# Opening of a hybrid transformer layer on one core: seven accumulators in place of six, mod sums and transposes in one PSUM bank, the second block's columns in three parts, six empty row steps

## The chip, the cores and the metric

One core of one Trainium2 chip runs the kernel. The metric is the device time of one execution in microseconds (us); the median of three executions of the kernel before the change is 1300.45 us (1300.31 to 1301.47). Lower is better.

## What is computed

One layer on x of 512 rows (T) and 1024 columns (D), float32 throughout. A conditioning vector c gives nine rows of modulation, `mod = silu(c) @ w_ada + b_ada`, 1024 wide each. Then come a SwiGLU feed-forward block (FFN, half weight), a mixer that adds a chunked matrix LSTM and a causal attention with forget gates, and a second FFN, each behind an RMS norm that is scaled and shifted by rows of `mod`.

```python
def swiglu(u, w_in, w_out):
    a, b = jnp.split(u @ w_in, 2, axis=-1)
    return (jax.nn.silu(a) * b) @ w_out
```

The change touches the first norm and the first FFN: `u = rms_norm(x) * gain * (1 + mod row 1) + mod row 0`, and `u @ w_in`, where `w_in` is 1024 by 2 x 2816 (an a half and a b half). The 2816 columns of a half are 22 blocks of 128, called j = 0 to 21.

## The kernel before, in words

**Products.** A float32 product is made of three products of rounded parts: a tensor u is split in `uh` (high part) and `ul` (the rest), a weight in `wh` and `wl`; `wh*uh`, `wl*uh` and `wh*ul` are added in a PSUM bank (PSUM is where TensorE writes). The high part is made on ScalarE (ACT in the profile), the rest on VectorE (DVE). PSUM has two pools of four banks, `gbank()` and `tbank()`.

**Opening** (`start`, L940 to L1106). It makes the first norm and the columns j = 0, 1, 2 of both halves, in eight blocks k of 128 rows of `w_in`, while everything is still being loaded. SyncE (SP) issues the loads in order: x, then for each k `ada_load(k)` (tile `ar`: the two column groups k of rows 0 and 1 of `w_ada`, four DMAs of 256 KB) and `load(k)` (tile `raw`: two DMAs of 192 KB). PE (TensorE) first runs `fill(30)`, thirty transposes of an identity matrix whose result nobody reads. For k = 0 the rows of `mod` are made on PE (`mod0`, L988, one call for each of the two rows), for k = 1 partly on PE (`mod1`, L994) and partly on DVE, from k = 2 on on DVE: `mod_first` (L998, L1000) and seven `mod` steps (L1003), each one of eight row blocks of `ar` times c, summed in the tile `ac`. `sums(k)` (L1018, two calls, four matmuls in the profile) adds the 128 partitions of `ac` on PE. `affine` (L1020, L1021, on ACT) makes the scale and shift `m` from these. `turn(k)` (L977) transposes the normed x into a bank `bt`; `u_hi` (L1026, L1028, ACT) reads it with `m` and writes `uh[k]` and `uf`; `u_lo` (L1030, DVE) writes `ul[k]`. Every one of these stands in the written order on its engine (`pin`).

The main loop runs k = 0 to 7. A block has 18 matmuls (L1084): three products, each into six accumulators, four `g` banks and two `t` banks. Between them stand, for the next k, `turn` ahead of the eighth matmul and `sums` ahead of the thirteenth. Of the two `t` banks left, one (`cb`) holds all sums, the results of `mod0` and the fill, and one holds `bt`.

**After the opening** (`run`). The six accumulators become three blocks of h. `ffn_in` then makes j = 3 alone, an a and a b half in a slot each of 24 matmuls (`w_stat`), and nine pairs of j in four slots each: 38 slots. Every `slot()` also runs one step of `pair_weights`, the later steps that are due (`tick`), and, if the slot's number n has n % 10 below 8, one step of `ada`: 32 steps, eight for each of the `mod` rows 3, 4, 2 and 6, each a load of 512 KB and one DVE step (L325) of about 1.2 us. After the eighth step of a row, `later` puts its end on the following ticks: `fold` (L364, L368), `high` (L369), `low` (L372), `total`, `bias` (L379) and `put`. The output product `pair_out` follows: eleven pairs, 18 matmuls each (two weight tiles, `wh`/`wl` of 1024 and of 512 columns), one tick in each pair.

The scheduler of the language sets the order on the engines outside the opening, from its own estimates.

Of the kernel before, what the change touches and what calls it, by code (L numbers as in the profile page):

```python
# [11 lines left out]
F32 = mybir.dt.float32  # L12
# [8 lines left out]
P = 128  # L21
# [26 lines left out]
class Layer:  # L48
# [359 lines left out]
    def ffn_in(self, w_in, j0, hp, tp, slot):  # L408

        if j0 % 2:  # L410
            ps = []
            for o in (0, FF):
                wt = self.w_stat(w_in, o + j0 * P)
                slot()
                ps.append(self.gbank())
                self.gemm_stat(ps[-1], wt, 0, T)
            self.pair_h(self.pair_s(ps[0], 0, T, tp), ps[1], j0, 0, T, hp, tp)
            self.lo_after = None
            j0 += 1
# [520 lines left out]
    def start(self, st, tp):  # L940
# [28 lines left out]
        def fill(n):  # L969

            for i in range(n):
                pin(nc.tensor.transpose(cb[:, 384:512], self.ident, self.ident))
# [5 lines left out]
        def ada_load(k):  # L978

            ars[k] = st.tile([P, NK, 2, P], F32, name=self.nm("ar"), tag="ar", bufs=7)  # L980
            halves = [(v, i) for v in range(2) for i in (0, 4)] if k == 0 else [(v, i) for i in (0, 4) for v in range(2)]
            for v, i in halves:
                nc.sync.dma_start(ars[k][:, i:i + 4, v, :], w_ada[i * P:(i + 4) * P, v * D + k * P:v * D + (k + 1) * P]
                                  .rearrange("(i p) n -> p i n", p=P))
        def mod0(v):

            for i in range(NK):
                pin(nc.tensor.matmul(cb[:, 128 * (v + 1):128 * (v + 2)], ars[0][:, i, v, :], self.ccol[:, i:i + 1].to_broadcast([P, P]),  # L988
                                     start=i == 0, stop=i == NK - 1))
# [14 lines left out]
        sh = [P, 2, NJ0 * P]  # L1004
        def load(k):
            raws[k] = self.raw(sh, [(lambda t, i=i: t[:, i, :],
                                     w_in[k * P:(k + 1) * P, i * FF:i * FF + NJ0 * P]) for i in range(2)])
# [5 lines left out]
        def w_lo(k):  # L1013
            hi, lo = ws[k]
            pin(nc.vector.tensor_tensor(lo, raws.pop(k), hi, op=SUB))
        def sums(k):
            for v in range(2):
                pin(nc.tensor.matmul(cb[:, 2 * k + v:2 * k + v + 1], accs[k][:, v, :], self.one, start=True, stop=True))  # L1018
        def affine(k, m, c, b):
            pin(nc.scalar.activation(m[:, 0:1], c[0], AF.Identity, bias=b[0]))  # L1020
            pin(nc.scalar.activation(m[:, 1:2], c[1], AF.Identity, scale=self.colC[:, 8 + k:9 + k], bias=b[1]))  # L1021
        def u_hi(k):
            m = sp.tile([P, 2], F32, name=self.nm("m"), tag="m", bufs=4)
            c = (cb[:, 2 * k:2 * k + 1], cb[:, 2 * k + 1:2 * k + 2]) if k else (cb[:, 128:129], cb[:, 256:257])
            affine(k, m, c, base if k == 1 else (self.colC[:, 16 + k:17 + k], self.colC[:, 24 + k:25 + k]))
# [3 lines left out]
        def u_lo(k):  # L1029
            self.last_ul = pin(nc.vector.tensor_tensor(self.ul[k], ufs[k], self.uh[k], op=SUB))  # L1030
        for k in range(3):
            ada_load(k)
            load(k)
# [4 lines left out]
        acc_ps = [self.gbank() for _ in range(4)] + [self.tbank() for _ in range(2)]  # L1038
        cb = self.tbank()
        fill(30)  # L1040
# [11 lines left out]
        mod0(0)  # L1052
        turn(0, (0, 1))
        turn(1, (0, 1))
        mod0(1)
        turn(0, (2, 3))
        mod1()
        w_hi(0)
        w_lo(0)
        u_hi(0)  # L1060
        mc, mb = [sp.tile([P, 2], F32, name=self.nm("m"), tag="m", bufs=4) for _ in range(2)]
# [4 lines left out]
        pin(nc.vector.tensor_copy(mc, acc_ps[-1][:, 0:2]))  # L1066
        affine(1, mb, (mc[:, 0:1], mc[:, 1:2]), (self.colC[:, 17:18], self.colC[:, 25:26]))
        u_lo(0)
        mod(1, 4, 8)
        w_lo(1)  # L1070
        mod_first(2, True)
        for k in range(NK):
# [4 lines left out]
            wh, wl = ws[k]  # L1077
            for i, (p, b) in enumerate((p, b) for p in range(3) for b in range(2 * NJ0)):
                if n < NK and i == 7:
                    turn(n, range(NT) if k else (2, 3))  # L1080
                if n < NK and i == 12:
                    sums(n)
                s = slice(b // 2 * P, (b // 2 + 1) * P)
                pin(nc.tensor.matmul(acc_ps[b], (wl if p == 1 else wh)[:, b % 2, s], self.ul[k] if p == 2 else self.uh[k],  # L1084
                                     start=k == 0 and p == 0, stop=k == NK - 1 and p == 2))
# [496 lines left out]
    def run(self):  # L1582
# [11 lines left out]
        with tc.tile_pool(name="f1t", bufs=1) as tp:  # L1594
# [5 lines left out]
            with tc.tile_pool(name="f1h", bufs=1) as hp:  # L1600
                for j in range(NJ0):
                    self.pair_h(self.pair_s(acc_ps[2 * j], 0, T, tp), acc_ps[2 * j + 1], j, 0, T, hp, tp)
                new = lambda: [tp.tile([P, D], F32, name=self.nm("acc"), tag="xn", bufs=1)]
# [4 lines left out]
                def slot():  # L1608
# [3 lines left out]
                    if n % 10 < 8:  # L1612
                        next(ada, None)
                    n += 1
                self.ffn_in(A["ffn1_w_in"][0], NJ0, hp, tp, slot)
# [298 lines left out]
```

## Time and profile before

| what | value |
|---|---|
| median of three executions | 1300.45 us |
| the profiled execution, own time | 1301.22 us |
| its span in the trace | 1299.4 us |
| PE busy | 1286.9 us, 99% |
| DVE busy | 982.2 us, 76% |
| ACT busy | 657.0 us, 51% |
| first matmul of block 0 of the opening | 16.80 us |
| first matmul of j = 3 | 59.05 us |
| second slot (j = 3, b half) | 64.62 us |

Times in the trace count from the start of the span. A row of a timeline has the start, the duration, the engine, the line, the output and input tiles, and how many instructions it groups; in square brackets stands how long the engine had been idle and what ended that. The duration of one matmul overlaps with the next one: the distance of two starts is what counts. A row of the chain of waits has the start, the length and what the time was spent on.

### The profile page before, as it was taken

What the parts mean: (1) busy time and instruction counts of PE and PEld (TensorE: products, weight loads), DVE (VectorE), ACT (ScalarE), POOL (GpSimd) and SP (SyncE); (2) the same over time, 40 slices, a digit from 0 to 9 for tenths busy, and PEclk for the clock granted to TensorE, in tenths of its full rate; (3) what the DMA queues carried; (4) which work ended last, traced back from release to release, by engine and by line L of the source; (5) the groups of instructions that cost most, each with busy time, mean ns of one, the idle gap of its engine ahead of it and who ended that gap; (6) DMA issues with size and microseconds to landing.
All of it is one profiled execution on the core that took longest, in us unless ns stands there. A gap on an engine that the chain in (4) does not pass through costs nothing.

```text
span 1299.4 us, 17819 instructions
## 1 busy us (share of the span) xinstructions
PE 1286.9 (99%) x6241; PEld 1079.9 (83%) x6241; DVE 982.2 (76%) x1764; ACT 657.0 (51%) x1086; POOL 34.9 (3%) x73
## 2 busy tenths in 40 slices
PE   7999999999999999999999999999999999999998
PEld 6788888887889888888888888888898888888887
DVE  6887786678788878999997866778977656535787
ACT  5623333266467656666575886344683223223741
POOL 1000000000010001000001100000000000000000
PEclk9999999999999999999999999999999999999999
DMA  9999998755865634545456985876649767634574
GB/s 291 274 311 304 328 308 276 227 175 178 303 193 140 178 100 130 172 137 158 133 128 163 269 192 141 245 233 201 194 149 333 274 229 270 219 98 139 166 268 148
DMA packets 248330, 272.02 MB, mean 209 GB/s; under 512 B 57824, under 2 KB 185472, under 8 KB 248240
## 3 DMA queue, kind: packets, MB, share of 16 engines
q1 hardware_dynamic: 241104, 254.55, 63.8%
q0 software_dynamic: 2752, 8.45, 1.9%
q10 hardware_dynamic: 4384, 7.88, 1.9%
q8 instruction: 49, 0.80, 0.3%
q14 instruction: 41, 0.34, 0.1%
HBM read 227.77 MB, written 43.06 MB: 208 GB/s over the span
## 4 chain that ended last, share of the span: by engine, by line
PE 90%; DVE 5%; DMA 2%; ACT 2%; issue 1%; SPq 1%; DVEq 0%; ACTq 0%
PE g L144 23%; PE g L142 23%; PE g L143 23%; PE t L142 4%; PE t L144 4%; PE t L143 4%; PE g L1084 1%; PE t L1500 1%; PE t L1470 1%; PE t L1440 1%; PE t L1441 1%; PE t L1084 1%; DVE wl L760 1%; DMA ar<-in_w_ada_dram 1%; ACT wh L117 0%
## 5 line engine op out<-in xcount | busy, mean ns | idle before, releaser
L117 ACT ACTIVATE wh<-raw 128x1024 fp32r<-128x1024 f32 (+2 forms) x238 | 239.9, 1015 | 350.3 <-DMA raw<-in_ffn_w_in_dram 116.6
L119 DVE TENSOR_TENSOR wl<-raw,wh 128x1024 fp32r<-128x1024 f32 (+2 forms) x238 | 276.6, 1168 | 137.1 <-ACT wh L117 128.5
L142 PE MATMUL g<-uh,wh 128*128 128x512 f32 (+1 forms) x880 | 341.1, 388 | 0.2 <-ACT wh L117 0.2
L144 PE MATMUL g<-uh,wl 128*128 128x512 f32 (+1 forms) x880 | 340.1, 386 | 0.3 <-DVE wl L119 0.2
L143 PE MATMUL g<-ul,wh 128*128 128x512 f32 (+1 forms) x880 | 339.2, 386 | 0.0
L144 PEld LDWEIGHTS g<-uh,wl 128*128 128x128 f32 x880 | 165.3, 188 | 34.2 <-DVE wl L119 0.9
L142 PEld LDWEIGHTS g<-uh,wh 128*128 128x128 f32 x880 | 165.4, 188 | 33.5 <-ACT wh L117 0.6
L143 PEld LDWEIGHTS g<-ul,wh 128*128 128x128 f32 x880 | 165.5, 188 | 32.4
L142 PE MATMUL g<-wh,uh 128*128 128x512 f32 (+1 forms) x256 | 97.6, 381 | 0.0
L144 PE MATMUL g<-wh,ul 128*128 128x512 f32 (+1 forms) x256 | 96.6, 377 | 0.0
L143 PE MATMUL g<-wl,uh 128*128 128x512 f32 (+1 forms) x256 | 96.5, 377 | 0.0
L325 DVE SCALAR_TENSOR_TENSOR acc<-raw,ccol,acc 128x1024 f32<-128x1024 f32 (+1 forms) x49 | 54.8, 1129 | 52.8 <-DMA raw<-in_w_ada_dram 52.8
L143 PE MATMUL t<-wl,A 128*128 128x512 f32 x176 | 68.5, 389 | 0.0
L142 PE MATMUL t<-wh,A 128*128 128x512 f32 x176 | 68.5, 390 | 0.0
L144 PEld LDWEIGHTS g<-wh,ul 128*128 128x128 f32 x256 | 48.2, 188 | 8.9
L143 PEld LDWEIGHTS g<-wl,uh 128*128 128x128 f32 x256 | 48.3, 189 | 8.3
L142 PEld LDWEIGHTS g<-wh,uh 128*128 128x128 f32 x256 | 48.2, 188 | 8.2
L142 PE MATMUL g<-yh,wh 128*128 128x512 f32 x128 | 50.0, 390 | 0.0
L144 PE MATMUL g<-yh,wl 128*128 128x512 f32 x128 | 49.9, 389 | 0.0
L143 PE MATMUL g<-yl,wh 128*128 128x512 f32 x128 | 49.8, 389 | 0.0
L1451 ACT ACTIVATE S<-S,mn 128x128 f32<-128x128 f32 (+1 forms) x64 | 35.6, 558 | 27.1 <-DVE mn L1443 17.0
L465 ACT ACTIVATE A<-E 128x768 fp32r<-128x768 f32 x22 | 18.6, 847 | 53.8 <-DVE E L464 53.6
(403 smaller groups left out, 2294.8 us busy)
## 6 DMA issues: line engine op xcount, KB each, us to landing
raw<-in_ffn_w_in_dram SPq DMA_DIRECT2D x80, 512.0 KB, 4.2
raw<-in_w_ada_dram SPq DMA_DIRECT2D x48, 512.0 KB, 5.7
raw<-in_w_mix_dram SPq DMA_DIRECT2D x46, 512.0 KB, 4.2
sa<-in_ffn_w_out_dram SPq DMA_DIRECT2D x22, 512.0 KB, 6.4
sb<-in_ffn_w_out_dram SPq DMA_DIRECT2D x44, 256.0 KB, 5.7
ws<-sa SPq DMA_DIRECT2D x22, 512.0 KB, 3.8
ws<-sb SPq DMA_DIRECT2D x44, 256.0 KB, 4.4
raw<-ws SPq DMA_DIRECT2D x44, 256.0 KB, 3.8
```

The costliest lines, as they stand in the source:

```text
L117: nc.scalar.activation(hi, src, AF.Copy)
L119: self.last_lo = nc.vector.tensor_tensor(lo, src, hi, op=SUB)
L142: pin(mm(ps, lh, rh, start=start, stop=False, skip_group_check=on))
L143: pin(mm(ps, lh, rl, start=False, stop=False, skip_group_check=on))
L144: self.last_mm = pin(mm(ps, ll, rh, start=False, stop=stop, skip_group_check=on))
L325: nc.vector.scalar_tensor_tensor(a, r[:, s], c, a, op0=MUL, op1=ADD)
L465: nc.scalar.activation(A1[:, 0:3, :], E[:, 0:3, :], AF.Copy)
L760: self.pin(self.nc.vector.tensor_tensor(l, self.raws[n][c], h, op=SUB))
L1084: pin(nc.tensor.matmul(acc_ps[b], (wl if p == 1 else wh)[:, b % 2, s], self.ul[k] if p == 2 else self.uh[k], start=k == 0 and p == 0, stop ...
L1440: nc.tensor.matmul(ps[:, :w], q[:, s], k[:, :w], start=True, stop=False)
L1441: nc.tensor.matmul(ps[:, :w], q[:, s], kl[:, :w], start=False, stop=True)
L1451: nc.scalar.activation(S[:, ws], S[:, ws], AF.Exp, scale=-1.0, bias=m, accum_out=sm[:, qb:qb + 1])
```

## The change

The opening now has seven accumulators, four `g` and three `t` banks. The seventh takes the a half of j = 3. `raw` of a block has 512 + 384 columns (128x896 in place of 128x768), so each k loads 64 KB more. Block 0 still has 18 matmuls; the seventh accumulator's three products of k = 0 stand first in block 1, which has 24; blocks 2 to 7 have 21. The bank `cb` is gone: `mod0` writes into accumulators 4 and 5, `mod1` and `sums(1)` into the seventh, and from k = 2 on `sums` takes a bank of the ring that `bt` also uses, of which one bank is left. So `sums(k)` needs the reads of the bank by `u_hi(k - 1)` done, and `turn(k)` those of `affine(k)`, which is issued right behind `sums`. `fill` has 25 transposes in a bank of that ring. `mod0` runs for both rows back to back, then `turn(0)` whole; `mod1` and what follows it (the copy, its `affine`, the DVE steps up to `mod_first(2)`) stand behind block 0's third matmul; `turn(1)` is whole and inside block 0. `sums` stands ahead of a block's own matmul 13 (k = 0), 10 (k = 1 and later; counted from 0, without the three extra), `turn` ahead of 8 (k = 0) and 15 (later). `ar` of k = 1 comes in six DMAs. After the opening, `ffn_in` makes only the b half of j = 3: 37 slots. The slots 8, 9, 18, 19, 28 and 29 have no `ada` step, so 31 of the 32 steps stand in slots, and the last one, of row 6, in the first tick of `pair_out`.

The diff, cut:

```diff
-    def ffn_in(self, w_in, j0, hp, tp, slot):
+    def ffn_in(self, w_in, j0, hp, tp, slot, s=None):
 
         if j0 % 2:
-            ps = []
-            for o in (0, FF):
-                wt = self.w_stat(w_in, o + j0 * P)
-                slot()
-                ps.append(self.gbank())
-                self.gemm_stat(ps[-1], wt, 0, T)
-            self.pair_h(self.pair_s(ps[0], 0, T, tp), ps[1], j0, 0, T, hp, tp)
+            wt = self.w_stat(w_in, FF + j0 * P)
+            slot()
+            ps = self.gbank()
+            self.gemm_stat(ps, wt, 0, T)
+            self.pair_h(s, ps, j0, 0, T, hp, tp)
...
-                pin(nc.tensor.transpose(cb[:, 384:512], self.ident, self.ident))
+                pin(nc.tensor.transpose(fb[:, 0:P], self.ident, self.ident))
...
-            halves = [(v, i) for v in range(2) for i in (0, 4)] if k == 0 else [(v, i) for i in (0, 4) for v in range(2)]
-            for v, i in halves:
-                nc.sync.dma_start(ars[k][:, i:i + 4, v, :], w_ada[i * P:(i + 4) * P, v * D + k * P:v * D + (k + 1) * P]
+            parts = [(0, 4), (4, 8)] if k != 1 else [(0, 4), (4, 6), (6, 8)]
+            for v, (i, e) in [(v, q) for v in range(2) for q in parts] if k == 0 else [(v, q) for q in parts for v in range(2)]:
+                nc.sync.dma_start(ars[k][:, i:e, v, :], w_ada[i * P:e * P, v * D + k * P:v * D + (k + 1) * P]
                                   .rearrange("(i p) n -> p i n", p=P))
...
             for i in range(NK):
-                pin(nc.tensor.matmul(cb[:, 128 * (v + 1):128 * (v + 2)], ars[0][:, i, v, :], self.ccol[:, i:i + 1].to_broadcast([P, P]),
+                pin(nc.tensor.matmul(acc_ps[4 + v][:, 0:P], ars[0][:, i, v, :], self.ccol[:, i:i + 1].to_broadcast([P, P]),
...
-        sh = [P, 2, NJ0 * P]
+        sh, na = [P, (2 * NJ0 + 1) * P], (NJ0 + 1) * P
         def load(k):
-            raws[k] = self.raw(sh, [(lambda t, i=i: t[:, i, :],
-                                     w_in[k * P:(k + 1) * P, i * FF:i * FF + NJ0 * P]) for i in range(2)])
+            raws[k] = self.raw(sh, [(lambda t, i=i: t[:, i * na:na + i * NJ0 * P],
+                                     w_in[k * P:(k + 1) * P, i * FF:i * FF + (NJ0 + 1 - i) * P]) for i in range(2)])
...
+        def affine(k, m, c, b, vs=(0, 1)):
+            for v in vs:
+                pin(nc.scalar.activation(m[:, v:v + 1], c[v], AF.Identity, bias=b[v],
+                                         **({"scale": self.colC[:, 8 + k:9 + k]} if v else {})))
         def sums(k):
+            c = self.tbank() if k > 1 else acc_ps[-1][:, 8:10]
             for v in range(2):
-                pin(nc.tensor.matmul(cb[:, 2 * k + v:2 * k + v + 1], accs[k][:, v, :], self.one, start=True, stop=True))
-        def affine(k, m, c, b):
-            pin(nc.scalar.activation(m[:, 0:1], c[0], AF.Identity, bias=b[0]))
-            pin(nc.scalar.activation(m[:, 1:2], c[1], AF.Identity, scale=self.colC[:, 8 + k:9 + k], bias=b[1]))
+                pin(nc.tensor.matmul(c[:, v:v + 1], accs[k][:, v, :], self.one, start=True, stop=True))
+            ms[k] = sp.tile([P, 2], F32, name=self.nm("m"), tag="m", bufs=6)
+            affine(k, ms[k], (c[:, 0:1], c[:, 1:2]), base if k == 1 else col(k))
         def u_hi(k):
-            m = sp.tile([P, 2], F32, name=self.nm("m"), tag="m", bufs=4)
-            c = (cb[:, 2 * k:2 * k + 1], cb[:, 2 * k + 1:2 * k + 2]) if k else (cb[:, 128:129], cb[:, 256:257])
-            affine(k, m, c, base if k == 1 else (self.colC[:, 16 + k:17 + k], self.colC[:, 24 + k:25 + k]))
+            m = ms[k]
             pin(nc.scalar.activation(self.uh[k], bt[k], AF.Identity, scale=m[:, 1:2], bias=m[:, 0:1]))
...
             self.last_ul = pin(nc.vector.tensor_tensor(self.ul[k], ufs[k], self.uh[k], op=SUB))
+        ms = {}
+        col = lambda k: (self.colC[:, 16 + k:17 + k], self.colC[:, 24 + k:25 + k])
...
-        acc_ps = [self.gbank() for _ in range(4)] + [self.tbank() for _ in range(2)]
-        cb = self.tbank()
-        fill(30)
+        fb = self.tbank()
+        fill(25)
+        acc_ps = [self.gbank() for _ in range(4)] + [self.tbank() for _ in range(3)]
...
-        mod0(0)
-        turn(0, (0, 1))
-        turn(1, (0, 1))
-        mod0(1)
-        turn(0, (2, 3))
-        mod1()
         w_hi(0)
         w_lo(0)
+        ms[0], mc, mb = [sp.tile([P, 2], F32, name=self.nm("m"), tag="m", bufs=6) for _ in range(3)]
+        c0 = [acc_ps[4 + v][:, 0:1] for v in range(2)]
+        mod0(0)
+        affine(0, ms[0], c0, col(0), (0,))
+        mod0(1)
+        affine(0, ms[0], c0, col(0), (1,))
+        turn(0, range(NT))
         u_hi(0)
-        mc, mb = [sp.tile([P, 2], F32, name=self.nm("m"), tag="m", bufs=4) for _ in range(2)]
         base = mb[:, 0:1], mb[:, 1:2]
...
         mod(1, 3, 4)
-        pin(nc.vector.tensor_copy(mc, acc_ps[-1][:, 0:2]))
-        affine(1, mb, (mc[:, 0:1], mc[:, 1:2]), (self.colC[:, 17:18], self.colC[:, 25:26]))
-        u_lo(0)
-        mod(1, 4, 8)
-        w_lo(1)
-        mod_first(2, True)
+        def mod1_out():
+            mod1()
+            pin(nc.vector.tensor_copy(mc, acc_ps[-1][:, 0:2]))
+            affine(1, mb, (mc[:, 0:1], mc[:, 1:2]), col(1))
+            mod(1, 4, 6)
+            u_lo(0)
+            mod(1, 6, 8)
+            w_lo(1)
+            mod_first(2, True)
         for k in range(NK):
...
                 load(k + 3)
-            wh, wl = ws[k]
-            for i, (p, b) in enumerate((p, b) for p in range(3) for b in range(2 * NJ0)):
-                if n < NK and i == 7:
-                    turn(n, range(NT) if k else (2, 3))
-                if n < NK and i == 12:
+            todo = [(p, b, k) for p in range(3) for b in range(2 * NJ0 + (k > 0))]
+            if k == 1:
+                todo = [(p, 2 * NJ0, 0) for p in range(3)] + todo
+            for i, (p, b, m) in enumerate(todo):
+                if k == 0 and i == 3:
+                    mod1_out()
+                if n < NK and i == (13, 13, 10)[min(k, 2)]:
                     sums(n)
-                s = slice(b // 2 * P, (b // 2 + 1) * P)
-                pin(nc.tensor.matmul(acc_ps[b], (wl if p == 1 else wh)[:, b % 2, s], self.ul[k] if p == 2 else self.uh[k],
-                                     start=k == 0 and p == 0, stop=k == NK - 1 and p == 2))
+                if n < NK and i == (8, 18, 15)[min(k, 2)]:
+                    turn(n, range(NT))
+                c = b % 2 * na + b // 2 * P
+                pin(nc.tensor.matmul(acc_ps[b], ws[m][p == 1][:, c:c + P], self.ul[m] if p == 2 else self.uh[m],
+                                     start=m == 0 and p == 0, stop=m == NK - 1 and p == 2))
...
+                s3 = self.pair_s(acc_ps[2 * NJ0], 0, T, tp)
...
-                    if n % 10 < 8:
+                    if n not in (8, 9, 18, 19, 28, 29):
                         next(ada, None)
                     n += 1
-                self.ffn_in(A["ffn1_w_in"][0], NJ0, hp, tp, slot)
+                self.ffn_in(A["ffn1_w_in"][0], NJ0, hp, tp, slot, s3)
+                self.later(1, lambda: next(ada, None))
```

On PE, the start of the opening up to the fourth matmul of block 0, before (`ar_158` is k = 0, `ar_166` k = 1, `t_302` and `t_305` are `bt` of k = 0 and 1):

```order
L988 MATMUL t_215<-ccol,ar_158 128x128 x8
L977 MATMUL t_302<-ident,xn_272 128x128
L977 MATMUL t_302<-ident,xn_274 128x128
L977 MATMUL t_305<-ident,xn_272 128x128
L977 MATMUL t_305<-ident,xn_274 128x128
L988 MATMUL t_215<-ccol,ar_158 128x128 x8
L977 MATMUL t_302<-ident,xn_290 128x128
L977 MATMUL t_302<-ident,xn_292 128x128
L994 MATMUL t_214<-ccol,ar_166 128x1 x4
L1084 MATMUL g_209<-uh_193,wh_322 128x512
```

And after (`t_317` is `bt` of k = 0):

```order
L986 MATMUL t_241<-ccol,ar_158 128x128 x8
L986 MATMUL t_242<-ccol,ar_158 128x128 x8
L975 MATMUL t_317<-ident,xn_270 128x128
L975 MATMUL t_317<-ident,xn_272 128x128
L975 MATMUL t_317<-ident,xn_288 128x128
L975 MATMUL t_317<-ident,xn_290 128x128
L1093 MATMUL g_237<-uh_195,wh_292 128x512
L1093 MATMUL g_238<-uh_195,wh_292 128x512
L1093 MATMUL g_239<-uh_195,wh_292 128x512
L992 MATMUL t_243<-ccol,ar_166 128x1 x4
```

The second `mod0` now stands ahead of all transposes of k = 0, those of k = 1 are gone from here, and `mod1` (L994, now L992) moved behind three matmuls of block 0.

On PE inside block 1, from the second product of the first accumulator to its third, before (sums of k = 2 in `ac_349`, bank `t_215` is `cb`, `t_420` is `bt` of k = 2):

```order
L1084 MATMUL g_209<-uh_194,wl_335 128x512
L977 MATMUL t_420<-ident,xn_272 128x128
L977 MATMUL t_420<-ident,xn_274 128x128
L977 MATMUL t_420<-ident,xn_290 128x128
L977 MATMUL t_420<-ident,xn_292 128x128
L1084 MATMUL g_210<-uh_194,wl_335 128x512
L1084 MATMUL g_211<-uh_194,wl_335 128x512
L1084 MATMUL g_212<-uh_194,wl_335 128x512
L1084 MATMUL t_213<-uh_194,wl_335 128x512
L1084 MATMUL t_214<-uh_194,wl_335 128x512
L1018 MATMUL t_215<-one,ac_349 128x1 x2
L1084 MATMUL g_209<-ul_202,wh_334 128x512
```

And after, from the third matmul of the second product on (sums in `t_424`, `bt` in `t_435`):

```order
L1093 MATMUL g_239<-uh_196,wl_326 128x512
L1021 MATMUL t_424<-one,ac_355 128x1 x2
L1093 MATMUL g_240<-uh_196,wl_326 128x512
L1093 MATMUL t_241<-uh_196,wl_326 128x512
L1093 MATMUL t_242<-uh_196,wl_326 128x512
L1093 MATMUL t_243<-uh_196,wl_326 128x512
L1093 MATMUL g_237<-ul_204,wh_325 128x512
L975 MATMUL t_435<-ident,xn_270 128x128
L975 MATMUL t_435<-ident,xn_272 128x128
L975 MATMUL t_435<-ident,xn_288 128x128
L975 MATMUL t_435<-ident,xn_290 128x128
L1093 MATMUL g_238<-ul_204,wh_325 128x512
```

The sums now stand ahead of the fourth matmul of the second product and of the transposes, which stand behind the first matmul of the third; six matmuls follow the transposes before block 2 begins, where before six followed the sums.

On DVE, in `pair_out` where the low part `hl` of row 6's fold is made, before (counting `pair_out`'s pairs from 0, `wl_2494` of 1024 and `wl_2500` of 512 columns are pair 3's, `wl_2539` is pair 4's):

```order
L119 TENSOR_TENSOR wl_2494<-raw_2490,wh_2493 128x1024
L372 TENSOR_TENSOR hl_2462<-acc_2060,hl_2462 64x1024
L458 TENSOR_TENSOR R_2359<-g_2290,sl_2287 128x512
L467 TENSOR_TENSOR R_2359<-E_2345 128x256
L463 TENSOR_TENSOR E_2345<-E_2345,R_2359 128x256
L119 TENSOR_TENSOR wl_2500<-raw_472_2497,wh_2499 128x512
L464 TENSOR_TENSOR E_2345<-E_2345 128x256
L397 COPY sh_2506<-g_2504 128x8
L468 TENSOR_TENSOR R_2359<-R_2359,E_2345 128x256
L398 SCALAR_TENSOR_TENSOR G_2507<-g_2504,colA 128x8
L119 TENSOR_TENSOR wl_2539<-raw_2535,wh_2538 128x1024
```

And after (the first row is pair 3's, `wl_2535` and `wl_2541` are pair 4's, `wl_2574` is pair 5's; `sh` and `G` are columns made of row 3):

```order
L119 TENSOR_TENSOR wl_2494<-raw_474_2491,wh_2493 128x512
L119 TENSOR_TENSOR wl_2535<-raw_2531,wh_2534 128x1024
L397 COPY sh_2499<-g_2497 128x8
L398 SCALAR_TENSOR_TENSOR G_2500<-g_2497,colA 128x8
L372 TENSOR_TENSOR hl_2503<-acc_2087,hl_2503 64x1024
L456 TENSOR_TENSOR R_2353<-g_2284,sl_2281 128x512
L465 TENSOR_TENSOR R_2353<-E_2339 128x256
L461 TENSOR_TENSOR E_2339<-E_2339,R_2353 128x256
L119 TENSOR_TENSOR wl_2541<-raw_485_2538,wh_2540 128x512
L462 TENSOR_TENSOR E_2339<-E_2339 128x256
L119 TENSOR_TENSOR wl_2574<-raw_2570,wh_2573 128x1024
```

All of pair 3's `wl` and the first tile of pair 4's now stand ahead of `hl`, where half of pair 3's stood ahead of it before: one pair more.

Further down on DVE, the last of ten steps L492 (L490 after) that end earlier parts of the product, before (`wl_2580` and `wl_2586` are pair 5's, `wl_2618` is pair 6's):

```order
L119 TENSOR_TENSOR wl_2580<-raw_2576,wh_2579 128x1024
L119 TENSOR_TENSOR wl_2586<-raw_492_2583,wh_2585 128x512
L492 TENSOR_TENSOR Ra_2608<-Ra_1349,A_495_2607 128x512
L492 TENSOR_TENSOR Rb_2609<-Rb_1350,A_495_2607 128x512
L119 TENSOR_TENSOR wl_2618<-raw_2614,wh_2617 128x1024
```

And after (`wl_2615` is pair 6's):

```order
L490 TENSOR_TENSOR Rb_2526<-Rb_994,A_479_2524 128x512
L490 TENSOR_TENSOR Ra_2564<-Ra_1165,A_488_2563 128x512
L490 TENSOR_TENSOR Rb_2565<-Rb_1166,A_488_2563 128x512
L490 TENSOR_TENSOR Ra_2605<-Ra_1338,A_498_2604 128x512
L490 TENSOR_TENSOR Rb_2606<-Rb_1339,A_498_2604 128x512
L119 TENSOR_TENSOR wl_2615<-raw_2611,wh_2614 128x1024
```

Pair 5's two `wl` have moved from between the ten steps to ahead of all of them; the ten now stand in one piece ahead of pair 6's. On PE, pair 5 before, and pair 6 after, begins with its L142 products alone, ahead of those that read `wl`.

## The prediction

> **What bounds the kernel now.** I read the page first: is any engine free to be made faster, or is one full?
>
> ```profile
> span 1299.4 us, 17819 instructions
> ...
> PE 1286.9 (99%) x6241; PEld 1079.9 (83%) x6241; DVE 982.2 (76%) x1764; ACT 657.0 (51%) x1086; POOL 34.9 (3%) x73
> ...
> PEclk9999999999999999999999999999999999999999
> ```
>
> PE is busy for all but 12.5 us, at the full granted clock. The change does not take a matmul of the FFN away: what six accumulators and the a half of j = 3 did, seven do. So it can win only where PE stands still or where matmuls follow each other more slowly, and it can lose wherever PE is made to wait. The second view is what PE waits for in the first 140 us.
>
> ```profile
> PE t L213 <- DMA rowsC<-in_b_ada_dram: 5.0, 1, 5.0
> PE t L1018 <- DVE ac L1003: 1.0, 2, 0.7
> PE t L988 <- DMA ar<-in_w_ada_dram: 0.3, 1, 0.3
> PE t L994 <- DMA ar<-in_w_ada_dram: 0.3, 1, 0.3
> ```
>
> The 5.0 us are the start, which the change leaves alone. Behind it PE waits for the steps on `ac` ahead of the sums, and for `ar`. PE's timeline (start, duration) shows where the front end stands, and how a block looks.
>
> ```profile
> 9.76 0.82 PE L972 MATMUL t<-ident 128*128 128x128 f32 x6
> 10.92 2.02 PE L988 MATMUL t<-ccol,ar 128*128 128x128 f32 x16 [0.34 <-DMA ar<-in_w_ada_dram]
> 12.78 0.60 PE L977 MATMUL t<-ident,xn 128*128 128x128 f32 x4
> 13.22 1.95 PE L988 MATMUL t<-ccol,ar 128*128 128x128 f32 x16
> 15.01 0.38 PE L977 MATMUL t<-ident,xn 128*128 128x128 f32 x2
> 15.44 0.61 PE L994 MATMUL t<-ccol,ar 128*128 128x1 f32 x4
> 16.33 0.61 PE L994 MATMUL t<-ccol,ar 128*128 128x1 f32 x4 [0.29 <-DMA ar<-in_w_ada_dram]
> 16.80 0.95 PE L1084 MATMUL g<-uh,wh 128*128 128x512 f32 x3
> ...
> 28.59 0.51 PE L1084 MATMUL g<-uh,wh 128*128 128x512 f32 x1
> ...
> 59.05 0.47 PE L142 MATMUL g<-uh,wh 128*128 128x512 f32 x1
> ...
> 64.62 0.39 PE L142 MATMUL g<-uh,wh 128*128 128x512 f32 x1
> ```
>
> Block 0 begins at 16.80, block 2 at 28.59, j = 3 at 59.05 and its b half at 64.62. The chain that ended last (start, length) tells what holds the early blocks and what the later ones.
>
> ```profile
> 16.71 7.17 DMA ar<-in_w_ada_dram
> ...
> 25.01 0.60 DVE ul L1030
> ...
> 26.58 0.61 PE t L1018 x4
> ...
> 31.63 0.46 PE t L1084 x2
> 32.09 0.36 PE t L1018 x4
> ...
> 33.95 1.10 PE g L1084 x4
> ...
> 49.66 1.11 PE g L1084 x4
> ```
>
> Up to 26.58 the end is set by the last piece of k = 2's `ar`, which lands at 16.71 + 7.17 = 23.88, and by DVE behind it (steps of `ac`, one `ul`): the sums follow 2.7 us after the landing. From there on PE sets it: three blocks from 33.95 to 49.66, 5.24 us each.
>
> **The change, part by part.** *First matmul.* `mod1`, two transposes of k = 1 and the pause between the halves of `mod1` leave the path. The second `mod0` follows the first at 12.78 in place of 13.22, 0.44 us sooner; its end goes from 15.01 to 14.57. The four transposes of k = 0 follow. ACT's `uh` for k = 0, which waits for the last of them (0.1 us each, as four in 0.44 above), then can end at about 16.0, where block 0 can begin at 16.05: 0.75 us sooner. Here the fill's cut costs nothing: at 0.14 us each (0.82 for six) five fewer add 0.7 us to a pause of 0.34, and `mod0` waits for its DMA either way.
>
> *Blocks 0 and 1.* Matmuls there stand 0.2315 us apart (two in 0.46 at 31.63); later it is 0.2267 (18 between 288.70 and 292.78, rows below). Block 0 has 18 of them (4.17), now with `mod1` (0.9, from its two rows without the pause), four transposes (0.44) and the sums (0.36, the chain's row at 32.09), 0.3 of restarts: it ends at 22.2. The three products of k = 0 for the seventh accumulator (0.69) lie in front of block 1 and hide the wait for `uh` of k = 1; block 1's own start is then 23.1. Its sums of k = 2 are due ten matmuls on, at 25.4.
>
> *The sums of k = 2.* Each k loads 64 KB more:
>
> ```profile
> DMA packets 8353, 4.92 MB, mean 308 GB/s; under 512 B 320, under 2 KB 8351, under 8 KB 8351
> ```
>
> This is the DMA from 14 to 30 us, full all the time. Two blocks' extra 131 KB at 308 GB/s are 0.43 us, so the piece lands at 24.3, and DVE's 2.7 us behind it make the sums start at 27.0. PE stands for 1.6 us, where it stood for 0.7 of the 1.0 above. Eleven matmuls (2.55), the transposes (0.44), the sums (0.36) and 0.2 bring block 2 to 30.55. Before it was 28.59, with six matmuls fewer done, worth 6 x 0.2267 = 1.36: **0.6 us lost**. The bounds come from DVE's row at that piece:
>
> ```profile
> 24.00 1.00 DVE L1003 SCALAR_TENSOR_TENSOR ac<-ar,ccol,ac 128x256 f32<-128x256 f32 x2 [1.06 <-DMA ar<-in_w_ada_dram]
> ```
>
> DVE stood 1.06 us for it. If it lands that much sooner, the term is a gain of 0.5; if the six DMAs of k = 1 and SP's two more issues push it back by half a us, a loss of 1.1.
>
> *Blocks 2 to 6.* ACT's rows show what ends a block before:
>
> ```profile
> 37.72 0.26 ACT L1020 ACTIVATE m<-t,colC 128x1 f32<-128x1 f32 x1 [1.05 <-PE t L1018]
> ...
> 38.26 0.78 ACT L1026 ACTIVATE uh<-t,m 128x512 fp32r<-128x512 f32 x1
> ...
> ACT uh L1026: 1.0, 3
> ```
>
> The sums, two small steps (from 37.72 to 38.26) and `uh` run after each other, 1.32 us against six matmuls (1.39) and a semaphore's way: PE waits for `uh` at each block's start. With `m` made early only `uh` (0.78) follows the transposes, and six matmuls hide it with 0.3 to spare. A block of 21 takes 21 x 0.2315 + 0.44 + 0.36 + 0.1 (restarts) = 5.75, against 5.24 + 3 x 0.2267 = 5.92 before: 0.17 gained in each of five, **0.85 gained**. If `uh` stays as late as now the term is zero. Block 7 has neither sums nor transposes, 21 x 0.2315 = 4.9. From 30.55 five blocks and this one end at 64.2, in place of 64.62; the 24 matmuls from 59.05 to 64.62 took 5.57, 0.13 over the later pace, which the first slot may pay again. I take 64.35: **0.3 gained** in all up to there.
>
> *The bank shared by sums and transposes.* A transpose now waits for `affine` to have read the sums. The two small steps take 0.54 us, and five matmuls (1.16) lie between: no cost, at most 0.2 per block. The Trainium skill, in PSUM — Partial Sum Buffer (PSUM bank collisions raise a hardware error), asks for just that guard: readers and TensorE are kept apart by whole bank, whatever the columns. No run before shows the wait; by the page alone a block would lose what the two steps and their semaphores exceed the five matmuls by, which is nothing here.
>
> *The FFN's slots and `pair_out`.* One slot and one step less of DVE, while PE waits for nothing between 64 and 268 us; so nothing is gained there. But the last step of row 6 and its fold come one pair later. DVE around it before:
>
> ```profile
> 276.85 1.22 DVE L372 TENSOR_TENSOR hl<-acc,hl 64x1024 fp32r<-64x1024 f32 x1
> ...
> 280.31 0.16 DVE L397 COPY sh<-g 128x8 f32<-128x8 f32 x1
> ...
> 288.27 1.82 DVE L119 TENSOR_TENSOR wl<-raw,wh 128x1024 fp32r<-128x1024 f32 x2
> 290.00 0.68 DVE L492 TENSOR_TENSOR Ra<-Ra,A 128x512 fp32r<-128x512 f32 x1
> ...
> 291.21 1.82 DVE L119 TENSOR_TENSOR wl<-raw,wh 128x1024 fp32r<-128x1024 f32 x2
> ```
>
> PE begins pairs 5 and 6 of `pair_out` with these rows:
>
> ```profile
> 288.70 0.62 PE L142 MATMUL t<-wh,A 128*128 128x512 f32 x2
> ...
> 292.78 0.39 PE L142 MATMUL t<-wh,A 128*128 128x512 f32 x1
> ```
>
> DVE runs without a pause from `hl` to pair 6's `wl`, whose 1024 columns are done at about 292.4: 15.55 us. A pair of PE takes 292.78 - 288.70 = 4.08. In the new order `hl` starts one pair later, at 280.9. Behind it come the same steps less one pair of `wl` (290.00 - 288.27 = 1.73) and less `sh` and `G` (0.2): 13.6, so pair 6's `wl` is done at 294.55. PE comes to pair 6 at 292.5 and has six L142 products (1.36) that need no `wl`: it waits from 293.85, **0.7 us lost**. Bounds: nothing, if `hl` is held only by half a pair; 2.0, if the fold takes one tick more on ACT as well.
>
> *Sum*, against the profiled execution's own 1301.22: - 0.3 for the opening (- 0.85 + 0.6, with the rounding of its ends) and + 0.7 for `pair_out`, 0.4 slower, 1301.6; this execution lies 0.77 above the median of 1300.45, so **1300.9** as a median. A measurement of this kernel can tell 0.2% (2.6 us) from no change; this is the same.
>
> **Rivals.** *Early data* (16%): the piece of `ar` lands 1.06 us sooner and `pair_out` hides its pair: 1300.9 - 1.1 - 0.7 = 1299.1. For it: DVE stood for this one piece of four. Against it: the bytes are more, not fewer.
>
> *PE-bound opening* (17%, faster): none of the waits is left. Then 168 matmuls at 0.2267 (38.1), `mod1` (0.9) and seven times transposes and sums (0.8, 5.6) from 16.05 end at 60.7, 3.9 before 64.62 in place of 0.3: 1297.3, or 1296.6 without `pair_out`'s 0.7. For it: from block 2 on PE alone is on the chain. Against it: the distance of 0.2315 in these blocks is PE's own pace there, and DVE's 2.7 us behind the DMA do not shrink.
>
> *Sums ahead of DVE* (10%, slower). From block 2 on the sums stand ten matmuls into a block, 2.3 us, where they stood twelve matmuls and the transposes in, 3.2. DVE must by then have made `ul` and two steps of `ac`, and `ul` waits for ACT's `uf`:
>
> ```profile
> 50.22 0.69 DVE L1030 TENSOR_TENSOR ul<-uf,uh 128x512 fp32r<-128x512 f32 x1 [0.28 <-ACT uf L1028]
> 50.83 1.00 DVE L1003 SCALAR_TENSOR_TENSOR ac<-ar,ccol,ac 128x256 f32<-128x256 f32 x2
> ```
>
> This block began at 49.6, so its `ac` is ready at 51.83, 2.2 us in: 0.1 to spare as things are, 0.4 if `uf` comes as much sooner as `uh`. It decides from the point where `uf` comes later than now; each block then pays in full, and so it is carried on. With `uf` 0.7 later, as in a block where ACT still makes `xn`, five blocks lose the 0.65 each and the 0.17 gained: 1300.9 + 4.1 = 1305.0.
>
> *Cold clock* (3%, slower): the pause ahead of `mod0` grows to 1.0 us. If PE's clock fell in it, the 32 matmuls of `mod0` would go at the pace of the fill's first ones: the first 24 took 9.76 - 5.24 = 4.52 us, 0.19 each, against 0.126 in `mod0`; with what follows until the clock is back some 3.5 us, 1304.4. Against it: the granted clock is full throughout, and the pause of 0.34 did nothing.
>
> ```profile
> 5.24 5.34 PE L972 MATMUL t<-ident 128*128 128x128 f32 x30
> ```
>
> The Trainium skill, in TensorE: Matmul & The Clock Gate (Part 1), says that the clock halves after an idle window of about 3.4 us and needs as long a busy one to come back. By that the 1.0 us here are too short; the slow first transposes agree with the second half of it.
>
> **How the numbers follow.** The forecast has 54%, 1300.9, with 1299.9 to 1302.2 of its own from the bounds of the sums and of `pair_out`. Early data lies within 0.2% too: same 0.70. The PE-bound opening gives faster 0.17, the two others slower 0.13. The range leaves out most of the PE-bound case and of the two slow ones: 1298.2 to 1303.2.
>
> **What would show it.** Right: block 0 near 16.05, one wait of about 1.6 us ahead of the sums of k = 2, blocks 2 to 6 in 5.75 without a wait for `uh`, the second slot's counterpart near 64.3, a wait of PE for `wl` (L119) near 293 to 295. Wrong: a wait at every sums (rival three), first `mod0` steps over 0.2 us apart (the clock), blocks of 5.4 us or less (PE-bound), no wait in `pair_out`.

## The result and the profile after

The changed kernel takes 1314.38 us (median of four executions, 1312.95 to 1316.53) against 1300.5 us for the kernel before: 1.0107 of its time, 95% interval 1.0089 to 1.0124. It is 13.9 us slower, and the forecast of 1300.9 (1298.2 to 1303.2) is wrong. The ratios and ranges below leave out one execution each of a_phase, b_late and the kernel before, which took hundreds of us longer.

The page of the changed kernel, the lines that answer to those of before:

```profile
span 1311.8 us, 17819 instructions
...
PE 1295.8 (99%) x6236; PEld 1082.9 (83%) x6236; DVE 981.7 (75%) x1763; ACT 655.2 (50%) x1085; POOL 34.5 (3%) x73
```

The span is 12.4 us longer, and 8.9 of these are PE being *busy* longer (1295.8 against 1286.9) with the same matmuls, but for five transposes fewer in the fill. Waits explain only the rest. The opening is not the place. Its timeline on PE:

```profile
16.34 0.97 PE L1093 MATMUL g<-uh,wh 128*128 128x512 f32 x3 [0.93 <-ACT uh L1026]
...
27.30 0.58 PE L1021 MATMUL t<-one,ac 128*128 128x1 f32 x4 [0.19 <-DVE ac L1001]
...
30.81 1.07 PE L1093 MATMUL g<-uh,wh 128*128 128x512 f32 x4
...
59.36 1.07 PE L1093 MATMUL g<-uh,wh 128*128 128x512 f32 x4
...
64.15 0.47 PE L142 MATMUL g<-uh,wh 128*128 128x512 f32 x1
```

Block 0 begins at 16.34, block 2 at 30.81, and five blocks on, block 7 at 59.36: 5.71 each. The b half of j = 3 begins at 64.15, 0.47 sooner than before. So the time is lost behind the opening. What PE waits for from 220 to 310 us:

```profile
PE g L142 <- ACT wh L117: 2.4, 1, 2.4
PE g L144 <- DVE wl L119: 0.9, 1, 0.9
PE t L143 <- DVE wl L119: 0.5, 1, 0.5
PE g L143 <- DVE wl L119: 0.2, 1, 0.2
```

Before, PE waited for nothing in this stretch. The wait of 2.4 stands in the first pair of `pair_out`; the chain of waits up to it, cut (start, length, what):

```profile
258.88 3.83 DMA raw<-in_w_ada_dram
...
262.81 0.06 DVE acc L325
...
264.01 1.23 DVE wl L119
...
265.26 0.33 SPq L107
...
265.64 0.42 SPq L107
...
266.11 5.44 DMA raw<-ws
...
271.64 0.64 ACT wh L117
```

A load of a `mod` row (L107, from `w_ada`) is issued at 258.88; only when DVE has used it (about 264.0) and has made the next `wl` (265.24) do SP's next two loads into the ring of `raw` go out, and behind these on SP's queue the first pair's own second weight (`raw<-ws`) is issued at 266.11; it lands at 271.55. Before, that weight was issued at 262.27. The table of stretches (us, PE busy, count, granted clock, DMA share, GB/s) shows what follows:

```profile
18.00:22.00 4.00, 4.00 (x14) 0.57 1.17 311
22.00:31.00 9.00, 8.81 (x45) 1.00 1.13 309
268.00:274.00 6.00, 3.33 (x14) 1.00 0.46 144
274.00:278.00 4.00, 4.00 (x13) 0.57 0.72 188
278.00:380.00 102.00, 101.53 (x434) 1.00 0.68 220
```

After the pause the granted clock is about half for 3.4 us (0.57 as a mean of 274 to 278), and it is so in block 0 too (18 to 22); before, it was 1.00 in both stretches. But from 278 to 380 the clock is full, PE is busy for 101.53 of 102 us, and still does less in a microsecond. Two rows 24 matmuls apart, in `pair_out`, of the kernel before:

```profile
341.62 0.39 PE L142 MATMUL t<-wh,A 128*128 128x512 f32 x1
...
347.06 0.39 PE L142 MATMUL t<-wh,A 128*128 128x512 f32 x1
```

And of the changed kernel:

```profile
343.51 0.40 PE L142 MATMUL t<-wh,A 128*128 128x512 f32 x1
...
349.11 0.40 PE L142 MATMUL t<-wh,A 128*128 128x512 f32 x1
```

5.44 us became 5.60: 0.2333 us per matmul for 0.2267, with the same instructions on the same shapes. The same holds in the second FFN's output product, a part of the program that the change does not touch. Two rows 24 matmuls apart there, before:

```profile
1237.60 0.39 PE L142 MATMUL t<-wh,A 128*128 128x512 f32 x1
...
1243.04 0.39 PE L142 MATMUL t<-wh,A 128*128 128x512 f32 x1
```

And after, again 5.60 us in place of 5.44:

```profile
1232.27 0.40 PE L142 MATMUL t<-wh,A 128*128 128x512 f32 x1
...
1237.87 0.40 PE L142 MATMUL t<-wh,A 128*128 128x512 f32 x1
```

### The profile page after: what moved, and what is told of

It reads as the page before. It is cut to its first block, busy times and chain, and to the rows that moved or that the text cites. A ratio compares the mean times of both kernels' runs of the same rounds, so it can differ in the third digit from the quotient of the medians.

```text
span 1311.8 us, 17819 instructions
## 1 busy us (share of the span) xinstructions
PE 1295.8 (99%) x6236; PEld 1082.9 (83%) x6236; DVE 981.7 (75%) x1763; ACT 655.2 (50%) x1085; POOL 34.5 (3%) x73
## 4 chain that ended last, share of the span: by engine, by line
PE 88%; DVE 5%; DMA 3%; ACT 2%; issue 1%; SPq 1%; POOL 0%; DVEq 0%; ACTq 0%; POOLq 0%
PE g L144 22%; PE g L143 22%; PE g L142 22%; PE t L143 4%; PE t L144 4%; PE t L142 4%; PE g L1093 1%; PE t L1509 1%; PE t L1479 1%; DVE wl L119 1%; PE t L1093 1%; DMA ar<-in_w_ada_dram 1%; PE t L1449 1%; PE t L1450 1%; ACT wh L117 0%
## 5 line engine op out<-in xcount | busy, mean ns | idle before, releaser
L142 PE MATMUL g<-uh,wh 128*128 128x512 f32 (+1 forms) x872 | 338.1, 388 | 0.3 <-ACT wh L117 0.3
L143 PE MATMUL g<-ul,wh 128*128 128x512 f32 (+1 forms) x872 | 336.1, 385 | 0.0
L142 PEld LDWEIGHTS g<-uh,wh 128*128 128x128 f32 x872 | 163.9, 188 | 32.8 <-issue 0.6
L143 PEld LDWEIGHTS g<-ul,wh 128*128 128x128 f32 x872 | 163.9, 188 | 32.3
L142 PE MATMUL g<-wh,uh 128*128 128x512 f32 (+1 forms) x256 | 97.8, 382 | 0.0
L143 PE MATMUL g<-wl,uh 128*128 128x512 f32 (+1 forms) x256 | 96.5, 377 | 0.0
L143 PE MATMUL t<-wl,A 128*128 128x512 f32 x176 | 70.2, 399 | 0.5 <-DVE wl L119 0.5
L142 PE MATMUL t<-wh,A 128*128 128x512 f32 x176 | 70.2, 400 | 0.0
L142 PEld LDWEIGHTS g<-wh,uh 128*128 128x128 f32 x256 | 48.2, 188 | 8.3
L143 PEld LDWEIGHTS g<-wl,uh 128*128 128x128 f32 x256 | 48.3, 189 | 8.3
L143 PE MATMUL g<-yl,wh 128*128 128x512 f32 x128 | 50.2, 392 | 0.0
L142 PE MATMUL g<-yh,wh 128*128 128x512 f32 x128 | 49.8, 389 | 0.0
```

The source lines that it names most:

```text
L142: pin(mm(ps, lh, rh, start=start, stop=False, skip_group_check=on))
L143: pin(mm(ps, lh, rl, start=False, stop=False, skip_group_check=on))
```

## The theories and the experiments

What reaches the second FFN is memory. The ring of small tiles `m` went from four to six, of 32 bytes each in a partition, so every tile allocated behind it lies 64 bytes higher, the stationary tiles `A` of both output products and the mixer's `yh` and `yl` among them. The weights' tiles `wh`, `wl` and `uh`, `ul` lie ahead of it and did not move. *Theory 1*: this displacement slows the matmuls that read a displaced tile beside one that stayed. *Theory 2*: the last row step in `pair_out` holds up the first pair's weights on SP and in the ring of `raw`. *Theory 3*, formed after a_addr_row5: the steps of the rows and of the stored weights stand one slot nearer to the FFN's end than before. The rivals: the pace comes from the changed order elsewhere; the late load is a matter of the DMA.

**Only the displacement, in the kernel before** (b_m6).

```diff
-            m = sp.tile([P, 2], F32, name=self.nm("m"), tag="m", bufs=4)
+            m = sp.tile([P, 2], F32, name=self.nm("m"), tag="m", bufs=6)
```

> The kernel before, with only the ring of the small tiles m made six deep in place of four, which moves every tile of SBUF that is allocated behind it (A of both output products, most of the mixer's) up by 64 bytes. Theory 1 (the 64 bytes make the matmuls that read these tiles slower): both output products at 0.234 us per matmul in place of 0.227, as in the changed kernel, about 3 us more in each and 1 to 1.5 in the mixer: 1307 to 1308 us. Rival (the pace comes from the changed order of other engines' work): 0.227 and 1300.5 us.

1306.49 us (1306.01 to 1307.69) beside 1300.19, ratio 1.0051 (1.0034 to 1.0068). The rows in `pair_out`, 24 matmuls apart:

```profile
342.72 0.39 PE L142 MATMUL t<-wh,A 128*128 128x512 f32 x1
...
348.32 0.39 PE L142 MATMUL t<-wh,A 128*128 128x512 f32 x1
```

5.60 us, as in the changed kernel. Six microseconds come from a number that allocates 64 bytes; for these the rival is out. The FFN's own products, whose two tiles (`uh` or `ul`, `wh` or `wl`) both lie ahead of the ring, keep their pace: from j = 3 to the first matmul of `pair_out` it is 208.41 us (59.15 to 267.56), before it was 208.35 (59.05 to 267.40).

**The changed kernel at the addresses of before** (a_addr): three of the small tiles share one.

```diff
-        ms[0], mc, mb = [sp.tile([P, 2], F32, name=self.nm("m"), tag="m", bufs=6) for _ in range(3)]
+        mq = sp.tile([P, 8], F32, name=self.nm("m"), tag="mq", bufs=1)
+        ms[0], mc, mb = [mq[:, 2 * i:2 * i + 2] for i in range(3)]
...
-            ms[k] = sp.tile([P, 2], F32, name=self.nm("m"), tag="m", bufs=6)
+            ms[k] = sp.tile([P, 2], F32, name=self.nm("m"), tag="m", bufs=3)
```

> The changed kernel, with the small tiles m packed so that they take as much as before (three of them in one tile, a ring of three), so that all tiles behind them lie at the addresses of before. Theory 1: the pace is 0.227 again, about 7 us less than the changed kernel: 1307 us. Rival: 1314 us, no change of pace.

1307.0 us (1304.71 to 1308.32), 7.4 less than the changed kernel, to the forecast microsecond. Rows 24 matmuls apart in `pair_out` are 5.44 us apart again (342.69 and 348.13). The waits stay about as they were:

```profile
PE g L142 <- ACT wh L117: 2.5, 1, 2.5
PE t L143 <- DVE wl L119: 0.7, 1, 0.7
PE g L144 <- DVE wl L119: 0.6, 1, 0.6
PE g L143 <- DVE wl L119: 0.2, 1, 0.2
```

**32 bytes up, 32 bytes down** (b_m5, b_m3): as b_m6, with `bufs=5` and `bufs=3`.

> The kernel before with a ring of five small tiles m: all tiles behind them 32 bytes up in place of 64. Theory 1 has no number for this distance: if any move away from the address of before costs, 0.23 us or more per matmul in both output products and 1303 to 1307 us; if what counts is the place within 64 bytes, something new; if only 64 bytes hurt, 1300.5.

> The kernel before with a ring of three small tiles m: all tiles behind them 32 bytes down. As for 32 bytes up: 1300.5 if only the distance of 64 hurts, 1303 to 1307 if any does. Up and down by 32 bytes differ by 64; if they come out alike, the rule is not a simple one of 128 bytes.

1308.45 us (1308.28 to 1308.86; ratio 1.0062, 1.0047 to 1.0077) and 1307.73 (1307.67 to 1308.08; 1.0056, 1.0039 to 1.0073). All three displacements that were tried cost 6 to 8 us. Not all matmuls suffer alike. Before, the mixer's three products had 389 or 390 ns. From 830 to 920 us, in the mixer (columns: count, busy us, mean ns), with 64 bytes (b_m6):

```profile
L142 PE MATMUL g<-yh,wh 128*128 128x512 f32 x115 | 45.3, 394 | 0.0
L144 PE MATMUL g<-yh,wl 128*128 128x512 f32 x115 | 45.1, 392 | 0.0
L143 PE MATMUL g<-yl,wh 128*128 128x512 f32 x115 | 44.7, 389 | 0.0
```

and with 32 up (b_m5):

```profile
L143 PE MATMUL g<-yl,wh 128*128 128x512 f32 x116 | 45.8, 395 | 0.0
L144 PE MATMUL g<-yh,wl 128*128 128x512 f32 x116 | 45.8, 395 | 0.0
L142 PE MATMUL g<-yh,wh 128*128 128x512 f32 x115 | 45.5, 396 | 0.0
```

At 32 bytes all three products have 395 or 396, where at 64 one keeps 389. Which one is not fixed: in the changed kernel, also at 64 bytes, it is `yh,wh`. Why one is spared stays open.

**Everything 64 bytes up** (b_all64): the weights and `uh` too, so that no distance between them changes.

```diff
-        self.one = cp.tile([P, 1], F32, name="one")
+        self.one = cp.tile([P, 24], F32, name="one")[:, 0:1]
```

> The kernel before with 64 bytes of padding ahead of everything: the small constants grow, so that u, the weights and all tiles behind move up together by 64 bytes and keep their distances. Theory 1a (what costs is the distance of the weights' tiles from the tiles A and y that are read beside them): 0.227 us per matmul and 1300.3 us. Theory 1b (a tile's own place within 128 bytes costs): all of it is now misplaced, the FFN's first products too, 0.23 us and more everywhere, 1307 us at least and up to 1335.

1301.04 us (1299.79 to 1301.61), ratio 1.0005 (0.9996 to 1.0014). Two rows of it 24 matmuls apart are 5.44 us apart:

```profile
341.27 0.39 PE L142 MATMUL t<-wh,A 128*128 128x512 f32 x1
...
346.71 0.39 PE L142 MATMUL t<-wh,A 128*128 128x512 f32 x1
```

So, at 64 bytes, it is the distance between tiles that costs, not a tile's own place; that the two are those which one matmul reads is argued from the products that kept their pace in b_m6. Why the distance counts, and what other distances would cost, no run shows.

**No step in the output product** (a_row5, and a_addr_row5 at the addresses of before).

```diff
-                    if n not in (8, 9, 18, 19, 28, 29):
+                    if n not in (8, 9, 18, 19, 28):
...
-                self.later(1, lambda: next(ada, None))
```

> The changed kernel with five empty slots in place of six, so that all 32 steps of the mod rows stand in the 37 slots and none in the output product. Theory 2 (the load of the last step takes a buffer of the ring that the first pairs' weights need, and stands ahead of theirs on SP's queue): the wait of 2.4 us for the first pair's second weight tile goes, and with it the stretch of half clock behind it (1.6 us) and the 0.5 us before the seventh pair: 4 to 5 us less, 1309.5 to 1310.5. Rival (that load is late because the FFN is a slot shorter, whatever the step): the wait stays, 1314 us.

> Both edits: the addresses of before and five empty slots. If the two theories hold and their parts add, 1314.4 - 7 - 4.5 = 1303 us, with what is left of the wait in the FFN (1.2 us near 246) and the half clock in block 0 (1.7 us). If one of the two fails, 1307 or 1310.

1310.09 us (1306.61 to 1310.35) and 1303.28 (1299.59 to 1305.55): 4.3 and 3.7 less, and the parts add. In the second:

```profile
PE g L144 <- DVE wl L119: 1.7, 1, 1.7
PE g L142 <- ACT wh L117: 0.5, 1, 0.5
PE g L143 <- DVE wl L119: 0.2, 1, 0.2
```

The first pair's wait fell from 2.5 to 0.5, the seventh pair's (t L143) is gone. Near 246, in the FFN, PE now waits 1.7 us, where it waited 0.6 in a_addr.

**The same edit the other way, in the kernel before** (b_late).

```diff
-                    if n % 10 < 8:
+                    if n % 10 < 8 and n < 37:
...
+                self.later(1, lambda: next(ada, None))
```

> The kernel before with the last step of row 6 taken from its last slot (number 37) and put into the first tick of the output product, nothing else. Theory 2: SP's queue holds the first pair's weights up in the same way, PE waits about 2 us for wh near 267 to 272, half a us before the seventh pair, perhaps with half clock behind it: 1303 to 1305 us. Rival: 1300.5.

A miss: 1301.17 us (median; 1300.94 to 1301.94), ratio 1.0006 (0.9996 to 1.0015). From 60 to 310 us PE has one wait:

```profile
PE t L143 <- DVE wl L119: 0.7, 1, 0.7
```

It is the seventh pair's, the 0.7 us of the forecast. The scheduler put the last row load at 252.19, and the first pair's weights behind it are in time. Theory 2 does not hold alone: the late step by itself costs 0.7 in this trace, too little for the comparison of times. The 2.4 us need something else of the change as well; that it is the missing slot is argued, not shown.

**Steps where they were, counted from the FFN's end** (a_phase, at the addresses of before).

```diff
                     next(pw, None)
-                    if n not in (8, 9, 18, 19, 28, 29):
+                    if n == 8:
+                        next(pw, None)
+                    if n not in (8, 17, 18, 27, 28):
                         next(ada, None)
...
-                self.later(1, lambda: next(ada, None))
```

> The changed kernel with the addresses of before, and with the steps of the mod rows and of the stored weights in the same places before the end of the FFN as in the kernel before: empty slots 8, 17, 18, 27, 28, and two steps of pair_weights in slot 8. Theory 3 (what is left over 1300 us comes from these steps standing one slot nearer to the end and meeting the DVE work of other pairs): the waits for wl near 229 and 246 and those at the start of the output product go, 2.5 to 3 us less than with five empty slots in their places (1303.3), so 1300 to 1300.5. Rival (a longer opening of the DMA's queue, nothing of the phase): 1303.

1300.21 us (median; 1298.90 to 1301.79), ratio 0.9998 (0.9988 to 1.0007); from 60 to 310 us:

```profile
PE g L142 <- ACT wh L117: 0.9, 1, 0.9
PE g L143 <- DVE wl L119: 0.2, 1, 0.2
PE g L144 <- DVE wl L119: 0.2, 1, 0.2
```

3.1 us less than a_addr_row5, as theory 3 said against its rival's 1303; the wait near 246 is gone. The edit moves both sorts of steps at once, so which of them counts is not shown. The waits up to 310 us explain 1.1 of the 3.1 (2.4 there, 1.3 here), and the two profiled spans differ by 1.5 (1301.5 and 1300.0); the rest lies in the spread of a_addr_row5 (1299.59 to 1305.55) or stays open.

**Towards a better kernel** (a_best1, a_best2, a_best3, each on top of the one before; the first on a_phase).

```diff
-                    if n not in (8, 17, 18, 27, 28):
+                    if n not in (8, 17, 18, 27):
...
-                if n < NK and i == (13, 13, 10)[min(k, 2)]:
+                if n < NK and i == (13, 17, 10)[min(k, 2)]:
-                if n < NK and i == (8, 18, 15)[min(k, 2)]:
+                if n < NK and i == (8, 19, 15)[min(k, 2)]:
...
         turn(0, range(NT))
+        for _ in range(6):
+            pin(nc.tensor.transpose(acc_ps[-1][:, P:2 * P], self.ident, self.ident))
```

> The changed kernel with the addresses of before, two steps of pair_weights in slot 8, and only four empty slots (8, 17, 18, 27), so that the rows' last step comes one slot sooner still. Theory 3: the two waits at the start of the output product (0.9 and 0.2 us) go as well: 1299.2 us. Rival: the denser loads make PE wait in the FFN, 1300 to 1301.

> As a_best1, and in block 1 the sums of k = 2 four matmuls later and the transposes one later, so that four more matmuls cover the wait for the sums (1.4 us there). If that wait is set by the last piece of ar as forecast, 0.9 us less at the sums, 0.2 given back between sums and transposes: 0.6 us less than a_best1, 1298.6.

> As a_best2, and six transposes of the identity whose result nobody reads between the transposes of k = 0 and block 0, in PE's wait of 0.9 us for uh, so that the granted clock does not fall in block 0 (18 to 22 us). If the half clock there follows from PE's pauses between 14 and 18 us, it is gone in most executions and the sums of k = 2 find their data at 27.1 either way: 1298 to 1299 us with less spread than a_best2 (1298.9 to 1301.6). Rival (the half clock comes from the pause ahead of mod0): no change, 1300 us.

1299.63 us (1299.02 to 1301.9; ratio 0.9999, 0.9990 to 1.0009), 1300.18 (1298.88 to 1301.63; 1.0000, 0.9991 to 1.0009) and 1299.58 (1298.92 to 1302.05; 0.9999, 0.9990 to 1.0008). In a_best1 all waits of the FFN and `pair_out` are gone. In a_best3 the mean granted clock is 1.00 in ten of eleven executions (in six of eleven of a_best1, in five of eleven of a_best2), and the wait for the sums is 0.4, where a_phase at full clock had 1.5:

```profile
PE t L213 <- DMA rowsC<-in_b_ada_dram: 5.5, 1, 5.5
PE t L986 <- DMA ar<-in_w_ada_dram: 0.6, 1, 0.6
PE t L1021 <- DVE ac L1001: 0.4, 1, 0.4
PE g L1096 <- ACT uh L1026: 0.3, 1, 0.3
```

That the six transposes keep the clock up is likely by these counts, but they are few. None of the three beats the kernel before by more than can be measured.

## Why the prediction was wrong, point by point

- *First matmul at 16.05*: right to 0.3. It was 16.34; PE waited 0.93 us for `uh`.
- *The sums of k = 2 at 27.0 after a wait of 1.6*: the time is right (27.30), the wait here 0.19. Half clock in block 0 had eaten it. With a full clock (a_phase) the sums began at 27.08, the wait was 1.5, and block 2 began at 30.59, only 0.2 sooner than here; DVE's steps on the last piece of `ar`, for which it had waited, began 0.2 sooner too (24.41 for 24.63). So the data set the end of that stretch, and the slow clock costs nothing there.
- *Blocks 2 to 6 in 5.75, without a wait for `uh`, end at 64.3*: 5.71, none, 64.15.
- *The shared bank costs nothing*: no wait of a transpose for `affine` shows in the blocks.
- *`pair_out`: the seventh pair waits 0.7*: right: 0.5 here (at 300.6, as all is later there), 0.7 in a_addr, and 0.7 in b_late at 293.8, where the forecast had it.
- *"One slot and one step less of DVE ... so nothing is gained there"*: the step that failed first. Nothing was gained, but the sentence priced the missing slot from PE's waits before and did not ask what the same steps would do one slot nearer to the end. I followed the late step on DVE and not on SP: its load and the ring of `raw` held the first pair's weights (2.4 us, about 1.6 more by half clock, with matmuls 0.43 us apart from 274.4 to 277.4), and the FFN lost some 1.2 us near 246. Together, with the seventh pair's wait, 6.8 us by the medians: a_addr 1307.0 less a_phase 1300.2 (5.7 by the spans of the profiles, 1305.7 and 1300.0).
- *The pace of 0.2267 taken as given*: the term that was not in the sum at all. 7.4 us by a_addr, 6.3 by b_m6 in the kernel before. The diff showed it, `bufs=4` to `bufs=6`, and I gave it no price.
- *The rivals*: early data did not come: the piece of `ar` came later than before (DVE's steps on it begin at 24.63, before at 24.00). Sums ahead of DVE did not happen. The PE-bound opening did not: the data of k = 2 hold it. The cold clock had 3% for a fall ahead of `mod0`, and a pause of 1.0 us was thought too short for it; half clock came instead in block 0, where the last pause was 0.93 us, and behind the first pair's wait of 2.4. None of the rivals reached a time near 1314.

The sum now: 1314.4 - 7.4 (distances) - 3.7 (last step, with the missing slot) - 3.1 (places of the steps) = 1300.2. These are the differences of four runs, each an edit on the one before, so they add up to a_phase by construction. The check on them is that the first comes to 6.3 in the other kernel (b_m6), and the second to 4.3 at the displaced addresses (a_row5). What the opening gains, 0.47 us, the waits of `pair_out` in a_phase (0.9 and twice 0.2) take back; without them (a_best1) a gain of that size, 0.04%, lies inside the interval of the comparison.

## What to carry to other kernels

A change that alters the size of a small SBUF tile can move all tiles behind it, as `m` did here: compare the matmuls' start-to-start pace in parts that the change does not touch, and if it differs at full clock, restore the addresses before judging the change. When a loop loses a slot, count its side steps from the end and not from the start, and follow each one's DMA through the queue and the ring that it shares with the next stage's first loads.

## What the runs showed of the hardware

- Matmuls of 128x512 in `pair_out` whose two tiles lay as before ran at 0.2267 us; with one of the two moved by 32 or 64 bytes, at 0.2333 (5.60 us for 24). With both moved by 64 they ran at 0.2267. Before, the tiles lay a multiple of 128 bytes apart; whether 128 is the period was not tried. Weight loads show 188 ns in both kernels, so they do not tell it. The mechanism stays open.
- The granted clock fell to about half for 3.4 us after a pause of 2.4 us of PE (0.43 us per matmul from 274.4 to 277.4), and in block 0 behind a last pause of 0.93 us (0.57 from 18 to 22 us) in the profiles of the changed kernel and of a_addr, but not in that of a_phase with the same opening (1.00, behind a pause of 0.93 too). The Trainium skill, in TensorE: Matmul & The Clock Gate (Part 1), names an idle window of about 3.4 us for it; here half clock followed shorter pauses, while its length agrees with the busy window that the page gives.
